# The token parts of a decoder's last gated projection: 384 and 160 columns instead of 256 and 288

## The chip, the cores and the metric

The kernel runs on one core of one Trainium2 chip. The time is device microseconds of that core, for one launch that does one inference step. The kernel before takes 2436.96 us (median of three runs, 2435.14 to 2437.22).

## What is computed

Two layers of a decoder trunk over 544 tokens (512 of a prompt, 8 x 4 of running samples), width 1024. A layer is a half-step SwiGLU, a mixer of three branches, a second half-step SwiGLU and a gated embedding. Only the last of these matters here, in the second layer, with the final norm behind it:

```python
h = rmsnorm(x, w['g_ple'])
x = x + jax.nn.sigmoid(h @ w['w_ple_gate']) * (p @ w['w_ple_proj'])
...
y_prompt = rmsnorm(yp, g_final)
y_sample = rmsnorm(ys, g_final)
```

`w_ple_gate` is 1024 x 1024, `w_ple_proj` is 256 x 1024, and `rmsnorm` divides each token by the root of its mean square over the 1024 channels.

## The kernel before

Activations lie transposed: channels on the 128 partitions, 544 tokens along the columns, in eight tiles `x[0]` to `x[7]`. Weights are blocks of 128 x 128 and are the stationary operand; the tokens stream. To keep f32 accuracy, every operand is split in a high and a low half (f32r), and a product is three matmuls that add up in PSUM: low weights with high tokens, high with high, high with low (`mm` in line 1066). Each of these matmuls is issued with a weight load of its own, also where two in a row use the same weights.

In most of the kernel a product streams the 544 tokens as two halves of 272 columns (lines 302 and 325). The last function, `ple_last` (from line 1053), instead takes the tokens in two parts, so that the final norm and the output of the first part can be done while the second part is computed. `parts` is in blocks of 128 tokens: (0, 2) is columns 0 to 255, (2, 5) is columns 256 to 543. It has these steps, each for a part `h` and a block of 128 output channels `m`:

- `gate(h, m)`: 8 blocks x 3 = 24 matmuls (line 1069), then VectorE multiplies by the norm (L1087) and ScalarE takes the sigmoid (L1088).
- `proj(h, m)`: 2 x 3 = 6 matmuls (L1069); VectorE multiplies with the gate (L1095) and adds to `x` (L1096); ScalarE squares the result (L1098, L1100); VectorE adds the squares up in `acc` (L1101).
- `norm_sum(h)`: for each block of 128 tokens a one-column matmul (L516, plain f32, two passes) sums `acc` over the partitions; a few tiny VectorE operations and a square root on ScalarE (L502, with a table load) make the inverse root; VectorE scales one identity block for each block of tokens (L523).
- `norm_bc(h)`: for each block a matmul with 128 columns (32 for the last) spreads the result over the partitions (L530, two passes); ScalarE copies it to `rstd` (L532, and L534 for the last 32 columns).
- `out(h, m)`: VectorE scales `x` (L1114) and a DMA on SP's or ScalarE's queue (L1116) writes the part's columns.

The order is written out by hand. Part 0: four gates interleaved, with the norm of the incoming `x` among them, then `proj(0, m)` and `gate(0, m + 4)` in turn, and the last four `proj`. Weights are split once, in part 0, and stay in SBUF for part 1. Part 1: `gate(1, 0)`, `gate(1, 1)`, `proj(1, 0)`, `gate(1, 2)`, `norm_sum(0)`, `proj(1, 1)`, `gate(1, 3)`, `norm_bc(0)`, `proj(1, 2)`, then the rest, two `out(0, ...)` behind each of four `proj`. At the end `norm_sum(1)`, `norm_bc(1)` and eight `out(1, m)`. PSUM is four tiles of two banks that are taken in turn (`bank`), so a group of matmuls must wait until the group four before it has been read.

Of the kernel before, what the change touches and what calls it, by code (L numbers as in the profile page):

```python
# [102 lines left out]
class Kern:  # L103
# [950 lines left out]
    def ple_last(self, l, inp):  # L1054
        nc = self.nc
        xg = inp.tiles
        pp, _ = self.pp_in
        self.extra = EXTRA[6]
        self.keep = True
        wg, wp, ts = {}, {}, {}  # L1060
        parts = ((0, 2), (2, 5))
        rms = {}

        def span(h):
            return slice(parts[h][0] * P, min(parts[h][1] * P, T))

        def mm(ps, w, xs, c, first, last):
            for i, (a, b) in enumerate(((w[1], xs[0]), (w[0], xs[0]), (w[0], xs[1]))):
                nc.tensor.matmul(ps, a, b[:, c], start=first and i == 0, stop=last and i == 2)  # L1069

        def acc_mm(h, store, name, m, xs):
            pst, = self.bank(1)
            c = span(h)
            ps = pst[:, 0, :c.stop - c.start]
            for k in range(len(xs)):
                if h == 0:
                    store[k, m] = self.take(name, l, k, m)
                mm(ps, store[k, m], xs[k], c, k == 0, k == len(xs) - 1)
            return ps

        def gate(h, m, ps=None):
            c = span(h)
            if ps is None:
                ps = acc_mm(h, wg, "w_ple_gate", m, xg)
            t_ = ts[h, m] = self.slot()
            t = t_[0][:, c]
            nc.vector.tensor_mul(t, ps, self.rstd[:, c])  # L1087
            nc.scalar.activation(t, t, AF.Sigmoid)  # L1088

        def proj(h, m):  # L1090
            c = span(h)
            ps = acc_mm(h, wp, "w_ple_proj", m, pp)
            t_ = ts.pop((h, m))
            t, x = t_[0][:, c], self.x[m][:, c]
            nc.vector.tensor_mul(t, ps, t)  # L1095
            nc.vector.tensor_add(x, x, t)  # L1096
            if m == 0:
                nc.scalar.activation(self.acc[:, c], x, AF.Square)  # L1098
            else:
                nc.scalar.activation(t, x, AF.Square)  # L1100
                nc.vector.tensor_add(self.acc[:, c], self.acc[:, c], t)  # L1101
            self.drop(t_)

        def norm_sum(h):
            rms[h], = self.bank(1)
            self.rms_sum(rms[h][:, 0, :], *parts[h])

        def norm_bc(h):
            self.rms_bc(rms[h], *parts[h])

        def out(h, m):
            c = span(h)
            t = self.slot()
            nc.vector.scalar_tensor_tensor(t[0][:, c], self.x[m][:, c], self.par[:, PB_GF + m:PB_GF + m + 1],  # L1114
                                           self.rstd[:, c], op0=ALU.mult, op1=ALU.mult)
            (nc.scalar if m % 2 else nc.sync).dma_start(out=self.outs["yT"][m][:, c], in_=t[0][:, c])  # L1116
            self.drop(t)

        c = span(0)
        pst = self.bank(2)  # L1120
        ps4 = [pst[i // 2][:, i % 2, :c.stop - c.start] for i in range(4)]
        hooks = dict(zip(LAST_AT, (f for _, f in self.rms_hooks())))
        for n in range(4 * KD):
            k, i = divmod(n, 4)
            wg[k, i] = self.take("w_ple_gate", l, k, i)
            mm(ps4[i], wg[k, i], xg[k], c, k == 0, k == KD - 1)
            if n in hooks:
                hooks[n]()
        self.flush()
        for m in range(4):  # L1130
            gate(0, m, ps4[m])
        for m in range(KD):
            proj(0, m)
            if m + 4 < KD:
                gate(0, m + 4)
        gate(1, 0)
        for m in range(KD):
            if m + 1 < KD:
                gate(1, m + 1)
            if m == 1:  # L1140
                norm_sum(0)
            if m == 2:
                norm_bc(0)
            proj(1, m)
            if 2 <= m < 6:
                out(0, 2 * m - 4)
                out(0, 2 * m - 3)
        norm_sum(1)
        norm_bc(1)
        for m in range(KD):  # L1150
            out(1, m)
# [120 lines left out]
```

## Time and profile before

| | |
|---|---|
| median of three runs | 2436.96 us |
| span of the profiled execution | 2435.3 us |
| TensorE matmuls busy | 2414.3 us |
| VectorE busy | 1903.0 us |
| ScalarE busy | 1087.3 us |
| weight loads and matmuls | 19016 each |
| of these, in `ple_last` (L1069) | 480: 240 of 256 columns, 240 of 288 |

The profile gives one time for the profiled execution, its span from the first to the last instruction; it lies 1.7 us below the median of the runs and 0.2 us above the shortest. Of the 2435.3 us, `ple_last` fills the last 80.5, from 2354.8 on. Busy times of TensorE are those of pipelined instructions with modelled ends: one matmul is shown with some 290 ns though the next one starts 125 ns later.

### The profile page before, as it was taken

The page shows a single profiled execution, that of the slowest core. Times are in us where ns is not written, and L with a number is a line of the kernel's source. Part 1 is how long each engine was busy: PE and PEld are TensorE (multiplying, and loading weights), DVE is VectorE, ACT ScalarE, POOL GpSimd, SP SyncE. Part 2 cuts the span into 40 slices and gives each one's busy share as a digit, 9 for nine tenths or more (in the row PEclk, how much of TensorE's full clock was granted, in tenths as well). Part 3 has the DMA queues.
Part 4 walks back from the last instruction along what each step waited for, and adds up shares of the span by engine and source line. Part 5 has one row for each costly group of instructions (what it writes and reads, how often), then busy time and mean ns, then how long its engine had stood idle before and what let it go on. Part 6 is the DMA issues. An engine that isn't in the chain of part 4 may idle for free.

```text
span 2435.3 us, 48371 instructions
## 1 busy us (share of the span) xinstructions
PE 2414.3 (99%) x19016; PEld 2401.5 (99%) x19016; DVE 1903.0 (78%) x3583; ACT 1087.3 (45%) x2021; POOL 202.0 (8%) x248
## 2 busy tenths in 40 slices
PE   8999999999999999999999999999999999999997
PEld 8999999999999999999999999999999999999997
DVE  7887776778788887878788777866788779877775
ACT  6443444444446444435554444434354454434352
POOL 1111000010110100100010110000011011101000
PEclk9999999999999999999999999999999999999998
DMA  6665551354554555555255565523455536656521
GB/s 199 143 148 140 148 163 58 88 143 118 145 158 114 141 144 145 148 139 157 63 139 142 135 157 137 161 70 82 128 133 146 165 91 145 157 131 154 145 80 38
DMA packets 173988, 318.79 MB, mean 131 GB/s; under 512 B 19584, under 2 KB 21888, under 8 KB 173760
## 3 DMA queue, kind: packets, MB, share of 16 engines
q1 hardware_dynamic: 139248, 252.24, 34.2%
q0 software_dynamic: 32640, 61.16, 15.0%
q8 instruction: 149, 2.44, 0.4%
q10 hardware_dynamic: 1872, 2.29, 0.3%
q14 instruction: 79, 0.65, 0.1%
HBM read 312.63 MB, written 2.99 MB: 130 GB/s over the span
## 4 chain that ended last, share of the span: by engine, by line
PE 99%; DVE 0%; ACT 0%; DMA 0%; issue 0%; DVEq 0%; ACTq 0%
PE ps L325 47%; PE ps L302 46%; PE ps L807 2%; PE ps L1069 2%; PE ps L530 0%; PE ps L516 0%; PE ps L972 0%; DMA par<-in_par 0%; DVE s L1114 0%; PE ps L974 0%; DVE x L1096 0%; ACT s L1100 0%; ACT L502 0%; ACT L244 0%; DVE s L1095 0%
## 5 line engine op out<-in xcount | busy, mean ns | idle before, releaser
L325 PE MATMUL ps<-s,s 128*128 128x272 f32 x9156 | 1162.0, 288 | 0.0
L325 PEld LDWEIGHTS ps<-s,s 128*128 128x128 f32 x9156 | 1153.5, 188 | 0.4 <-DVE s L938 0.2
L302 PE MATMUL ps<-s,s 128*128 128x272 f32 x8880 | 1132.6, 288 | 7.3 <-ACT s L443 7.3
L302 PEld LDWEIGHTS ps<-s,s 128*128 128x128 f32 x8880 | 1121.7, 189 | 7.6 <-ACT s L443 7.2
L244 ACT ACTIVATE s<-s 128x512 fp32r<-128x512 f32 x1169 | 663.1, 621 | 506.0 <-DVE s L237 461.6
L249 DVE TENSOR_TENSOR s<-s,s 128x512 fp32r<-128x512 f32 x1169 | 768.3, 685 | 8.6 <-ACT s L244 8.6
L231 POOL DMA_DIRECT2D s<-in_wts x218 | 186.0, 854 | 1738.2 <-DMA s<-in_wts 448.5
L660 DVE SCALAR_TENSOR_TENSOR x<-ps,x 128x544 f32<-128x544 f32 x128 | 92.4, 722 | 137.2 <-PE ps L302 137.0
L579 ACT ACTIVATE s<-ps 128x272 f32<-128x272 f32 x109 | 43.2, 396 | 251.3 <-PE ps L325 251.1
L237 DVE TENSOR_TENSOR s<-s,s 128x512 f32<-128x512 f32 x218 | 149.3, 685 | 0.0
L581 DVE TENSOR_TENSOR s<-ps,s 128x272 f32<-128x272 f32 x109 | 48.0, 441 | 69.5 <-PE ps L325 43.3
L587 DVE TENSOR_TENSOR s<-ps,s 128x272 f32<-128x272 f32 x109 | 48.1, 441 | 63.8 <-PE ps L325 62.7
L607 ACT ACTIVATE s<-s 128x544 f32<-128x544 f32 x88 | 57.9, 658 | 89.4 <-DVE s L620 89.0
L613 ACT ACTIVATE s<-s 128x544 fp32r<-128x544 f32 x88 | 57.6, 654 | 59.8 <-DVE s L610 44.1
L864 DVE TENSOR_TENSOR s<-ps,s 128x544 f32<-128x544 f32 x48 | 34.8, 725 | 50.7 <-PE ps L302 46.2
L616 DVE TENSOR_TENSOR s<-s,s 128x544 fp32r<-128x544 f32 x88 | 63.2, 718 | 5.9 <-ACT s L613 5.8
L1069 PE MATMUL ps<-s,s 128*128 128x256 f32 (+1 forms) x480 | 61.6, 289 | 1.8 <-ACT rstd L532 1.8
L623 DVE TENSOR_TENSOR s<-s,rstd 128x544 f32<-128x544 f32 x88 | 63.2, 718 | 0.1
L1069 PEld LDWEIGHTS ps<-s,s 128*128 128x128 f32 x480 | 60.5, 188 | 2.0 <-ACT rstd L532 2.0
L610 DVE TENSOR_TENSOR s<-s,s 128x544 f32<-128x544 f32 x82 | 58.9, 718 | 0.4
L858 ACT ACTIVATE s<-s 128x544 f32<-128x544 f32 x48 | 29.0, 652 | 67.6 <-DVE s L593 67.6
L620 DVE TENSOR_TENSOR s<-s,rstd 128x544 f32<-128x544 f32 x82 | 59.0, 719 | 0.0
(133 smaller groups left out, 1176.4 us busy)
## 6 DMA issues: line engine op xcount, KB each, us to landing
s<-in_wts SPq DMA_DIRECT2D x951, 256.0 KB, 3.4
s<-in_wts POOLq DMA_DIRECT2D x218, 256.0 KB, 4.6
x<-in_xT ACTq DMA_DIRECT2D x4, 272.0 KB, 5.2
x<-in_xT SPq DMA_DIRECT2D x4, 272.0 KB, 4.8
s<-in_pT POOLq DMA_DIRECT2D x4, 272.0 KB, 3.2
out_yT<-s SPq DMA_DIRECT2D x4, 144.0 KB, 1.8
out_yT<-s ACTq DMA_DIRECT2D x4, 144.0 KB, 1.8
s<-in_st_in POOLq DMA_DIRECT2D x2, 272.0 KB, 3.1
```

The lines of the kernel that those rows point to most:

```text
L231: self.nc.gpsimd.dma_start(out=t, in_=src(1 if w == "R1" else 2, 4), accum_op=ALU.add)
L237: self.nc.vector.tensor_add(self.new_raw(w, u0, 2 if w == "R3" else 1), self.read_raw(a, u0), self.read_raw(b, u0))
L244: self.nc.scalar.activation(a[0][:, :UC], self.read_raw(w, u0), AF.Copy)
L249: self.nc.vector.tensor_sub(lo, self.read_raw(w, u0), hi.bitcast(F32))
L302: self.nc.tensor.matmul(ps[:, h, :HT], a, bh, start=first and i == 0, stop=last and i == 2)
L325: self.nc.tensor.matmul(ps, a, b, start=first and i == 0, stop=last and i == 2)
L610: nc.vector.tensor_mul(o[:, :], o[:, :], t[:, :])
L616: nc.vector.tensor_sub(lo, o[:, :], hi.bitcast(F32))
L620: nc.vector.tensor_mul(t[:, :], t[:, :], self.rstd[:, :])
L623: nc.vector.tensor_mul(o[:, :], o[:, :], self.rstd[:, :])
L660: nc.vector.scalar_tensor_tensor(xm, self.pv(pst[i]), 0.5, xm, op0=ALU.mult, op1=ALU.add)
L1069: nc.tensor.matmul(ps, a, b[:, c], start=first and i == 0, stop=last and i == 2)
```

## The change

One table of two pairs: the border between the token parts moves by one block of 128 tokens. Part 0 is now columns 0 to 383, part 1 columns 384 to 543.

```diff
         wg, wp, ts = {}, {}, {}
-        parts = ((0, 2), (2, 5))
+        parts = ((0, 3), (3, 5))
         rms = {}
```

The number of matmuls and weight loads and their order stay. What changes are the widths of all operations in `ple_last` and the number of blocks in the two norms. Two places on TensorE show it. The first is `norm_sum(0)`, between `gate(1, 2)` (ahead) and `proj(1, 1)` (behind), before:

```order
-L1069 MATMUL ps_71<-s_4614_29706,s_4583_29519 128x288
-L1069 MATMUL ps_71<-s_4615_29707,s_4583_29519 128x288
-L516 MATMUL ps_72<-ones,acc 128x1 x2
-L1069 MATMUL ps_73<-s_4548_29348,s_4592_29560 128x288
-L1069 MATMUL ps_73<-s_4548_29348,s_4591_29559 128x288
```

At the same place with the change (`s_...` are SBUF slots, `ps_71` to `ps_74` the four PSUM tiles):

```order
+L1069 MATMUL ps_71<-s_4614_29706,s_4583_29519 128x160
+L1069 MATMUL ps_71<-s_4615_29707,s_4583_29519 128x160
+L516 MATMUL ps_72<-ones,acc 128x1 x3
+L1069 MATMUL ps_73<-s_4548_29348,s_4592_29560 128x160
+L1069 MATMUL ps_73<-s_4548_29348,s_4591_29559 128x160
```

The first norm sums three blocks instead of two, at the same place between the same neighbours, whose slots and PSUM tiles are the same. The second place is the end of TensorE's work, the last projection and the second norm, before:

```order
-L1069 MATMUL ps_72<-s_4551_29354,s_4622_29737 128x288
-L1069 MATMUL ps_72<-s_4552_29355,s_4622_29737 128x288
-L516 MATMUL ps_73<-ones,acc 128x1 x3
-L530 MATMUL ps_73<-s_4650_30393,ones 128x128 x2
-L530 MATMUL ps_73<-s_4650_30393,ones 128x32
```

And with the change:

```order
+L1069 MATMUL ps_72<-s_4551_29354,s_4622_29737 128x160
+L1069 MATMUL ps_72<-s_4552_29355,s_4622_29737 128x160
+L516 MATMUL ps_73<-ones,acc 128x1 x2
+L530 MATMUL ps_73<-s_4650_30395,ones 128x128
+L530 MATMUL ps_73<-s_4650_30395,ones 128x32
```

The last norm has two blocks instead of three. Each of these rows of L516 and L530 is two weight loads and two matmuls on the chip.

## Rows read from the trace of the kernel before

**Rows 1.** The page: span; TensorE's share; granted clock in 40 slices

```profile
span 2435.3 us, 48371 instructions
...
PE 2414.3 (99%) x19016; PEld 2401.5 (99%) x19016; DVE 1903.0 (78%) x3583; ACT 1087.3 (45%) x2021; POOL 202.0 (8%) x248
...
PEclk9999999999999999999999999999999999999998
```

**Rows 2.** Stages of `ple_last`: length, busy (count) by engine, granted clock, DMA

```profile
2354.80:2385.40 30.60, 30.60 (x262) 30.60 (x261) 17.08 (x43) 12.10 (x25) 0.00 (x0) 1.00 0.01 2
2385.40:2395.60 10.20, 10.20 (x79) 10.20 (x79) 5.21 (x13) 2.59 (x6) 0.00 (x0) 1.00 0.00 0
2395.60:2403.30 7.70, 5.97 (x47) 5.73 (x45) 4.30 (x15) 4.40 (x8) 0.00 (x0) 1.00 0.01 2
2403.30:2420.40 17.10, 17.03 (x126) 16.80 (x126) 10.35 (x24) 3.43 (x8) 0.00 (x0) 1.00 0.18 62
2420.40:2435.30 14.90, 2.93 (x12) 2.71 (x12) 7.06 (x22) 2.85 (x6) 0.00 (x0) 0.57 0.23 79
```

**Rows 3.** Timeline, matmuls of four widths: start, us, engine, line, operands, count

```profile
2354.84 4.76 PE L1069 MATMUL ps<-s,s 128*128 128x256 f32 x39
...
2339.80 10.44 PE L302 MATMUL ps<-s,s 128*128 128x272 f32 x82
...
433.65 27.22 PE L807 MATMUL ps<-s,s 128*128 128x512 f32 x117
...
2403.33 17.03 PE L1069 MATMUL ps<-s,s 128*128 128x288 f32 x126 [1.76 <-ACT rstd L532]
```

**Rows 4.** Timeline, narrow matmuls and their weight loads; last, the load after the hole

```profile
2359.33 1.20 PEld L516 LDWEIGHTS ps<-ones,acc 128*128 128x128 f32 x10
...
665.43 1.05 PE L972 MATMUL ps<-wst,s 128*128 128x128 f32 x8
...
2403.33 0.30 PEld L1069 LDWEIGHTS ps<-s,s 128*128 128x128 f32 x2 [2.00 <-ACT rstd L532]
```

**Rows 5.** Window of the spatial matmuls (128 and 32 columns), as rows 2

```profile
665.30:671.00 5.70, 5.70 (x43) 5.06 (x41) 5.06 (x12) 2.52 (x4) 0.00 (x0) 1.00 0.07 12
```

**Rows 6.** Timeline, ScalarE around the first part's norm

```profile
2396.91 1.28 ACT L502 ACT_TABLE_LOAD   x1
...
2401.27 1.28 ACT L1088 ACT_TABLE_LOAD   x1
...
2402.91 0.37 ACT L532 ACTIVATE rstd<-ps 128x256 f32<-128x256 f32 x1
```

**Rows 7.** Timeline of the tail

```profile
2418.81 0.46 DVE L1087 TENSOR_TENSOR s<-ps,rstd 128x288 f32<-128x288 f32 x1 [0.45 <-PE ps L1069]
...
2423.41 1.44 PE L516 MATMUL ps<-ones,acc 128*128 128x1 f32 x6 [3.05 <-DVE acc L1101]
...
2426.67 1.49 PE L530 MATMUL ps<-s,ones 128*128 128x128 f32 x6 [1.82 <-DVE s L523]
...
2428.70 3.52 DVE L1114 SCALAR_TENSOR_TENSOR s<-x,par,rstd 128x288 f32<-128x288 f32 x8 [1.74 <-ACT rstd L534]
2429.68 2.91 ACTq L1116 DMA_DIRECT2D out_yT<-s  x4
```

**Rows 8.** Groups from 2300 on, by shape: count, busy us, mean ns, idle before

```profile
L1096 DVE TENSOR_TENSOR x<-x,s 128x288 f32<-128x288 f32 x8 | 3.7, 459 | 0.3
...
L1114 DVE SCALAR_TENSOR_TENSOR s<-x,par,rstd 128x288 f32<-128x288 f32 x8 | 3.5, 511 | 1.7 <-ACT rstd L534 1.7
L1114 DVE SCALAR_TENSOR_TENSOR s<-x,par,rstd 128x256 f32<-128x256 f32 x8 | 3.5, 480 | 0.0
L1096 DVE TENSOR_TENSOR x<-x,s 128x256 f32<-128x256 f32 x8 | 3.4, 425 | 0.3
...
L1100 ACT ACTIVATE s<-x 128x288 f32<-128x288 f32 x7 | 3.1, 443 | 7.2 <-DVE x L1096 7.2
...
L1100 ACT ACTIVATE s<-x 128x256 f32<-128x256 f32 x7 | 2.9, 419 | 7.2 <-DVE x L1096 7.2
```

## The prediction, made before the change was run

> **What bounds the kernel now.** Read the page first: TensorE is busy for 99% of the span, and the granted clock stands at full speed in all slices but the last [rows 1]. So the time is the number of matmuls times the pace of one, plus the few stretches in which TensorE waits. The second view is the table by stage of the last function [rows 2]: part 0 (256 columns) fills 30.6 us without a gap, part 1 (288 columns) follows from 2385.4, there is one hole of 1.7 us (7.70 us with 5.97 busy, where the first part's norm is made), and from 2420.4 on a tail of 14.9 us in which TensorE does 2.93 us of work. The third view is the timeline of TensorE alone, for the pace of a matmul by its width [rows 3]. A matmul's own duration (280 to 300 ns) is latency; the pace is (busy time less one duration) divided by (count less one). For 256 columns (4.76 - 0.28)/38 = 118 ns; for 272, (10.44 - 0.29)/81 = 125 ns; for 288, (17.03 - 0.30)/125 = 134 ns; for 512, (27.22 - 0.39)/116 = 231 ns. From 256 to 512 this is close to a straight line, 0.44 ns a column. If it were straight for all widths, 384 + 160 columns would cost what 256 + 288 cost.
>
> The question is whether it stays straight below 256, and the fourth view answers that: what narrow matmuls cost when each brings its own weights [rows 4]. The loads for ten one-column matmuls take (1.20 - 0.19)/9 = 112 ns each; eight matmuls of 128 columns run at (1.05 - 0.27)/7 = 111 ns. One column and 128 columns cost the same: the 128x128 weight load sets the pace, not the columns. Those are plain f32 operands. For the operands of this projection there is one look: after the hole the first weight load has nothing before it, and two loads together take 0.30 us, the second itself 0.19, so the second began 0.11 us behind the first (last row of rows 4), at a time when no earlier matmul could hold it up. So a load takes some 110 ns here too; at 256 columns (118 ns) it is only just hidden, at 160 columns it is not.
>
> **The change, part by part.** The same 480 matmuls and weight loads run in the same order; the order of the instructions shows only other widths, and that the first norm takes three blocks of 128 tokens instead of two and the last one two instead of three.
>
> *Part 0, 240 matmuls from 256 to 384 columns.* No row has 384. Per column the 256 row gives 0.462 ns and the 512 row 0.452, so it lies between 173.5 and 177.3 ns; I take the straight line between both, 175. The stage also holds the 20 matmuls of the incoming norm at 112 ns, 2.2 us, which stay. Before: 30.6 us. After: 240 x 0.175 + 2.2 = 44.2. **+13.6 us** (13.2 to 14.2). Nothing hides it: TensorE has no gap in this stage. VectorE (17.1 us busy of 30.6) and ScalarE (12.1) grow with the columns by less than half and stay under 44.
>
> *Part 1 up to the norm, 78 matmuls from 288 to 160 columns* (two gates of 24, the first projection of 6, the third gate of 24). Streaming 160 columns would, on the line, take 118 - 96 x 0.44 = 76 ns; the load takes 112. The larger counts. I take 112 (108 to 115, the 0.11 us of the first load and a little for the hand-over). 10.2 us become 78 x 0.112 = 8.7, **-1.5**. VectorE enters this stage late, since each of the last four projections of part 0 leaves it and ScalarE a chain of some 2.2 us at 384 columns (three operations of 0.56 and a square of 0.53, on the line of the widths in [rows 8]) while TensorE needs only 4.2 us for all four; but it reads their PSUM tiles some 8.4 us after the last gate of part 0, and TensorE wants the last of them back only after 10.2 us (4.2 + 48 x 0.112 + 6 x 0.112). That cover is 1.8 us.
>
> *The hole.* It is set by ScalarE, not by matmuls: the table load for the square root, the root, the small VectorE chain, the scaled identity blocks, one projection step, the second table load, the sigmoid and the copy of the norm out of PSUM, which TensorE waits for [rows 6]. The two table loads of 1.28 us stay. One more block for the norm adds 0.22 us to its sums and 0.24 to the blocks; the copy grows from 256 to 384 columns, about 0.1; five steps of VectorE and ScalarE shrink from 288 to 160 columns. From [rows 8] such a step goes from 0.46 to 0.32 us on VectorE (459 at 288, 425 at 256: 1.06 ns a column) and from 0.44 to 0.34 on ScalarE (443 and 419). 7.7 us become about 7.2, **-0.5**; TensorE still waits some 1.7 us of it.
>
> *Part 1 after the norm to the last gate, 114 matmuls.* They take 15.5 us now, from 2403.33 to the VectorE step that reads the last gate at 2418.81 [rows 7], at 134 ns each and with the first load and the last latency around them. Each becomes 112: 114 x 0.022 = **-2.5**. VectorE must keep up: a step of 30 matmuls will take 3.35 us. Its work in it is four operations with the wait for the square, 0.35 + 0.35 + 0.36 + 0.35 with their issue, from 0.67 us behind the gate on, and in three of them two output scalings of 384 columns (480 at 256, 511 at 288: about 0.60 at 384, overlapped to 0.52 [rows 8]): some 3.1 us. Just covered; if not, at most 3 x 0.3 = 0.9 us come on top.
>
> *The tail*, from that VectorE step at 2418.81 to the end of the span, 16.5 us. The gate's product and two projection steps run in a row on VectorE and ScalarE: 4.6 us to the first norm matmul at 2423.41; with 160 columns 0.67 for the six matmuls of the first projection and eight operations of 0.32 to 0.35, 3.4 in all: -1.2. The sums: 4 matmuls instead of 6; they run at 0.21 us, since the mean granted clock of the stage is 0.57, so most of it at the lower level, 1.2 GHz, after TensorE stood idle: -0.4. The broadcast: 4 instead of 6, likewise -0.4. The copy to SBUF: -0.1. The eight last scalings: 3.52 us at 288, spaced 0.43; at 256 spaced 0.40, so at 160 about 0.30 with 0.39 for the last: 2.5, -1.0. The last transfer's landing: 80 KB instead of 144, at most -0.1. With the hand-overs between them **-3.3** (2.8 if the landing and the copy give nothing and the steps shrink less; 3.8 if the clock stays up because TensorE idles for a shorter time before the sums).
>
> Sum: 13.6 - 1.5 - 0.5 - 2.5 - 3.3 = **+5.8 us**. The profiled execution has a span of 2435.3 us, 1.7 below the median of the runs, 2436.96; I take the 1.7 as common to both kernels and put the sum on the median: **2442.8 us**, 0.24% more.
>
> A rule that speaks against this sum: the Trainium skill, page "TensorE: Matmul & The Clock Gate", section "Back-to-back issue gap", gives 81 ns at 128 columns and 131 ns at 512 for a stream of weight load and matmul pairs; an estimate from these two puts 160 columns at 85 ns, and the kernel near the next rival's time. The trace of this case does not agree: it has 231 ns at 512 and 111 at 128 [rows 3, 4].
>
> **The rivals.**
> (a) *The weight load is hidden at 160 columns after all*, because loads of this operand type run ahead in a steady stream and the 0.11 us after the hole was the latency of a first load. Then the pace is 76 ns. Up to the norm 78 x 0.076 = 5.9, -4.3; the hole stays with ScalarE, -0.5; after the norm TensorE would need 2.3 us a step and VectorE's 2.8 to 3.1 would bind: three steps of 2.8 and one of 2.3 give 10.7 instead of 15.1, -4.4; tail -3.3. Sum 13.6 - 12.5 = +1.1: 2438.1 us, no change. This is the case in which it is not slower; it decides from a load time under about 80 ns. For it: the plain f32 rows are another operand type. Against it: 0.11 us for the one load of this type that stands alone.
> (b) *The granted clock falls to 1.2 GHz in part 1*, at the hole or before it. At that level a pair takes 0.21 us (six take 1.44 us in [rows 7]); 228 matmuls would cost 22 us more, 2465 us. Against it: eight-packs of 128 columns with small gaps ran for 5.7 us at a granted clock of 1.00 [rows 5], and so did the hole of 1.7 us.
> (c) *VectorE becomes the bound* after the norm, by its two wide scalings a step, or the PSUM tiles come back late at the border of the parts (cover 1.8 us): up to 0.9 + 1 us more, 2444.7 us. For it: the margin of 0.2 us a step. Against it: PSUM has four tiles in turn, so a late step is made good by the three without scalings.
>
> **How the numbers follow.** Forecast 0.80, (a) 0.13, (b) 0.04, (c) 0.03. About 0.2% (4.9 us) is what a measurement of this kernel can tell from no change, and the forecast's own range, 2441.0 to 2444.6 (384 columns at 173.5 or 177.3 ns, loads at 108 or 115, tail 2.8 or 3.8, not all at one end together), crosses it: of its 0.80 I put 0.60 above and 0.20 within. With (b) and (c) slower, (a) mostly within: slower 0.67, same 0.31, faster 0.02. The range for 8 in 10 takes in (a) and (c) but not (b): 2437.6 to 2445.0 us.
>
> **What would show it.** In the profile after: the 384-column stretch at 175 ns a matmul and 44 us long; the 160-column stretch at 110 to 114 ns with weight loads back to back, whatever the columns; the hole still there and still ended by the copy of the norm; a tail of 13.2 us from the last gate's product. Wrong would be: a pace under 90 ns at 160 columns (rival a), a granted clock under 1.00 before the last matmul (b), TensorE waiting for VectorE's reads of PSUM in part 1 (c), or 384 columns off the line.

## The result, and the profile after

| | before | the change |
|---|---|---|
| median of five runs | 2436.96 us | 2454.64 us |
| lowest and highest | 2435.14, 2437.22 | 2441.82, 2454.79 |
| ratio, 95% interval | | 1.0063 [1.0045, 1.0082] |

The change is slower, outside the predicted range, and its runs do not scatter about a middle: one took 2441.82 us, four took 2454.50 to 2454.79. The profiled execution is the one of 2441.82 us, with a span of 2440.1. It is the one that shows what the columns do; what the other four did is not in it. The page of this profile, against [rows 1]:

```profile
span 2440.1 us, 48371 instructions
...
PE 2421.6 (99%) x19016; PEld 2409.0 (99%) x19016; DVE 1903.3 (78%) x3583; ACT 1086.6 (45%) x2021; POOL 201.4 (8%) x248
...
PEclk9999999999999999999999999999999999999999
```

TensorE has 7.3 us more busy time, VectorE and ScalarE the same; the clock row has no 8 left in the last slice. The stages of the last function in the same execution, against [rows 2] (length, busy time and count by engine, granted clock, DMA):

```profile
2354.00:2398.20 44.20, 44.20 (x261) 44.20 (x261) 20.61 (x44) 13.60 (x25) 0.00 (x0) 1.00 0.00 1
2398.30:2406.80 8.50, 8.50 (x78) 8.50 (x78) 5.25 (x12) 2.48 (x6) 0.00 (x0) 1.00 0.00 0
2406.80:2414.20 7.40, 5.68 (x51) 5.53 (x50) 3.67 (x16) 4.15 (x8) 0.00 (x0) 1.00 0.01 2
2414.30:2428.30 14.00, 14.00 (x126) 14.00 (x126) 9.12 (x24) 2.49 (x8) 0.00 (x0) 1.00 0.30 108
2428.30:2440.10 11.80, 2.06 (x11) 1.69 (x9) 5.41 (x21) 2.53 (x6) 0.00 (x0) 0.62 0.20 62
```

Part 0 takes 44.2 us instead of 30.6, part 1 and the tail are shorter, the hole (7.4 us with 5.68 busy) is still there, and the clock is at 1.00 until the tail. The timeline of this execution gives the paces and the steps of the tail, against [rows 3, 7] (start, us, engine, line, operands, count):

```profile
2353.95 7.01 PE L1069 MATMUL ps<-s,s 128*128 128x384 f32 x39
...
2406.96 0.76 PE L516 MATMUL ps<-ones,acc 128*128 128x1 f32 x6
...
2414.26 14.30 PE L1069 MATMUL ps<-s,s 128*128 128x160 f32 x126 [1.78 <-ACT rstd L532]
...
2427.26 0.32 DVE L1087 TENSOR_TENSOR s<-ps,rstd 128x160 f32<-128x160 f32 x1 [0.20 <-PE ps L1069]
...
2430.72 0.74 PE L516 MATMUL ps<-ones,acc 128*128 128x1 f32 x4 [2.16 <-DVE acc L1101]
...
2434.77 2.46 DVE L1114 SCALAR_TENSOR_TENSOR s<-x,par,rstd 128x160 f32<-128x160 f32 x8 [1.40 <-ACT rstd L534]
```

384 columns run at (7.01 - 0.34)/38 = 176 ns, 160 columns at (14.30 - 0.27)/125 = 112 ns.

### The profile page after: what moved, and what is told of

It reads as the page before. It is cut to its first block, busy times and chain, and to the rows that moved or that the text cites. A ratio compares the mean times of both kernels' runs of the same rounds, so it can differ in the third digit from the quotient of the medians.

```text
span 2440.1 us, 48371 instructions
## 1 busy us (share of the span) xinstructions
PE 2421.6 (99%) x19016; PEld 2409.0 (99%) x19016; DVE 1903.3 (78%) x3583; ACT 1086.6 (45%) x2021; POOL 201.4 (8%) x248
## 4 chain that ended last, share of the span: by engine, by line
PE 99%; DVE 0%; ACT 0%; DMA 0%; issue 0%; ACTq 0%; DVEq 0%
PE ps L325 47%; PE ps L302 46%; PE ps L1069 3%; PE ps L807 2%; PE ps L516 0%; PE ps L530 0%; PE ps L972 0%; DMA par<-in_par 0%; PE ps L974 0%; DVE s L1114 0%; ACT L502 0%; ACT L244 0%; ACT s L1100 0%; DVE x L1096 0%; DVE s L523 0%
## 5 line engine op out<-in xcount | busy, mean ns | idle before, releaser
L302 PE MATMUL ps<-s,s 128*128 128x272 f32 x8880 | 1132.0, 288 | 7.0 <-ACT s L443 7.0
L302 PEld LDWEIGHTS ps<-s,s 128*128 128x128 f32 x8880 | 1121.1, 189 | 7.3 <-ACT s L443 7.0
L613 ACT ACTIVATE s<-s 128x544 fp32r<-128x544 f32 x88 | 57.5, 654 | 59.7 <-DVE s L610 44.2
L1069 PE MATMUL ps<-s,s 128*128 128x384 f32 (+1 forms) x480 | 70.2, 307 | 1.8 <-ACT rstd L532 1.8
```

Of the source, the lines that this page charges most:

```text
L302: self.nc.tensor.matmul(ps[:, h, :HT], a, bh, start=first and i == 0, stop=last and i == 2)
```

## The experiments

All ran with the kernel before beside them, on one chip per group of runs; its runs there lie between 2435.7 and 2437.9 us. Each run is one execution.

| label | edit | runs | times, us | ratio to the kernel before, 95% interval |
|---|---|---|---|---|
| e1, with the first five | the change as it is | 12 | 4 at 2441.8 to 2442.1; 8 at 2452.7 to 2454.9 | e1: 1.0049 [1.0032, 1.0067] |
| e2 | no hole | 11 | 2440.6 to 2442.4 | 1.0020 [1.0011, 1.0029] |
| e3 | part 1 streams 256 columns | 7 | 6 at 2443.1 to 2443.4; 2444.5 | 1.0027 [1.0017, 1.0037] |
| e4 | part 1 streams 224 columns | 8 | 6 at 2442.0 to 2442.4; 2 at 2444.0 | 1.0024 [1.0014, 1.0033] |
| e5, e10 | one gate behind the hole streams 256 | 15 | 5 at 2441.9 to 2442.4; 10 at 2443.7 to 2444.9 | 1.0025 [1.0016, 1.0035], 1.0029 [1.0018, 1.0041] |
| e6 | all gates and projections but one ahead of the hole stream 256 | 6 | 3 at 2443.0 to 2443.3; 3 at 2452.6 to 2455.5 | 1.0047 [1.0030, 1.0063] |
| e7 | the kernel before | 10 | 2436.7 to 2438.0 | 1.0001 [0.9991, 1.0010] |
| e8 | the kernel before without the hole | 11 | 2434.5 to 2435.6 | 0.9991 [0.9983, 1.0000] |
| e9 | as e8, one DMA on another queue | 11 | 2434.1 to 2435.0 | 0.9991 [0.9982, 1.0000] |

### The change once more (e1)

No edit.

> The change once more, without an edit, to see how its executions spread. Theory A (the granted clock falls to 1.2 GHz at the hole in part 1, where TensorE waits for the copy of the first norm, and stays there for the matmuls of 160 columns behind it): the executions fall in two groups, one near 2441.8 us and one about 126 x (0.213 - 0.112) = 12.8 us above it, near 2454.6, and a trace of the second group shows 112 ns a pair up to the hole and 213 ns from it to the end. Theory B (the narrow stretch itself makes the clock fall, at a place of its own, with no need of the hole): the times lie spread between 2441 and 2465 us, and a trace shows the pace change to 213 ns away from the hole.

Seven runs: 2441.99, 2442.00, 2442.10 and 2452.67, 2454.73, 2454.73, 2454.85 us. This time the profiled execution is one of the upper group, span 2453.0. Its stages (the third is the hole, the fourth the 126 matmuls behind it):

```profile
2398.70:2407.30 8.60, 8.60 (x79) 8.60 (x79) 5.26 (x12) 2.48 (x6) 0.00 (x0) 1.00 0.00 0
2407.30:2414.60 7.30, 5.60 (x51) 5.44 (x49) 3.67 (x16) 4.15 (x8) 0.00 (x0) 1.00 0.01 2
2414.80:2441.60 26.80, 26.80 (x126) 26.78 (x126) 9.44 (x24) 2.73 (x9) 0.00 (x0) 0.50 0.16 59
2441.60:2453.00 11.40, 2.27 (x9) 1.85 (x8) 5.09 (x20) 2.20 (x6) 0.00 (x0) 0.50 0.19 58
```

And its TensorE timeline around the hole:

```profile
2408.00 3.56 PE L1069 MATMUL ps<-s,s 128*128 128x160 f32 x30
...
2412.02 0.88 PE L1069 MATMUL ps<-s,s 128*128 128x160 f32 x6
2414.66 27.13 PE L1069 MATMUL ps<-s,s 128*128 128x160 f32 x126 [1.76 <-ACT rstd L532]
```

Its last function begins 0.4 us later; from there to the end of the hole it takes what the other execution took, to a few hundredths: 30 matmuls in 3.56 us, a wait of 1.76 us for the copy of the norm. Behind the hole the granted clock is 0.50, that is 1.2 GHz, and it stays there until the end, though TensorE has no further gap in those 26.8 us. The pairs take (27.13 - 0.42)/125 = 214 ns instead of 112: 126 x 0.102 = 12.8 us, and the two spans differ by 12.9. So this execution of the upper group is one of the lower group with the clock lost behind the hole. Theory A's numbers hold; whether the hole or the narrow matmuls do it is for the next runs.

### The change without the hole (e2)

```diff
         def norm_bc(h):
+            if h == 0:
+                rms[h], = self.bank(1)
             self.rms_bc(rms[h], *parts[h])
...
-            if m == 2:
+            if m == 3:
                 norm_bc(0)
             proj(1, m)
-            if 2 <= m < 6:
-                out(0, 2 * m - 4)
-                out(0, 2 * m - 3)
+            if 3 <= m < 7:
+                out(0, 2 * m - 6)
+                out(0, 2 * m - 5)
```

> The change with the hole taken away: the broadcast of the first norm takes a PSUM tile of its own and comes one projection later, so that no group of matmuls waits for the copy; the outputs of part 0 follow one step later. Theory A: TensorE runs through part 1 without a gap, the clock stays at 1.00 up to the last projection, all executions are near 2441.8 - 1.8 = 2440 us. Theory B: the hole's 1.8 us are saved, but executions above 2450 us remain, most of them as with the change, and their mean granted clock is below 0.995.

Eleven runs, none above 2442.4 us. The stage table of its part 1 and two rows of its timeline:

```profile
2399.00:2427.00 28.00, 28.00 (x253) 28.00 (x252) 16.99 (x50) 9.35 (x21) 0.00 (x0) 1.00 0.12 41
2427.00:2440.20 13.20, 2.34 (x11) 1.96 (x9) 6.47 (x23) 2.53 (x6) 0.00 (x0) 0.62 0.26 85
```

```profile
2427.96 1.14 DVE L1116 SCALAR_TENSOR_TENSOR s<-x,par,rstd 128x384 f32<-128x384 f32 x2
...
2430.48 1.02 PE L516 MATMUL ps<-ones,acc 128*128 128x1 f32 x4 [3.22 <-DVE acc L1101]
```

28.0 us with 253 matmuls (the 240 of 160 columns, the twelve of the norm and the last of part 0) without a gap and at a clock of 1.00. So the narrow matmuls do not make the clock fall by themselves, in any of eleven runs; theory B is out. The 2 us expected did not show in the time, though. The outputs moved one step later, two scalings of 384 columns (1.14 us) now stand between VectorE's last two projections, and TensorE waits 3.22 us for the last sums where it waited 2.16. The sums take 1.02 us instead of 0.74, all of them at a granted clock of 0.50, which costs another 0.3. And the last function begins 0.7 us later in this execution than in the profiled one of the change (2354.66 against 2353.95), which has nothing to do with the edit (see e7).

### More columns in all of part 1 (e3, e4)

The parts stay; the matmuls of part 1 stream the last 256 (224) of the 544 columns, and the product that is read is the last 160 of these. The first 96 (64) are computed a second time and dropped.

```diff
             c = span(h)
+            if h == 1:
+                c = slice(T - 256, T)
             ps = pst[:, 0, :c.stop - c.start]
...
-            return ps
+            return pst[:, 0, 96:256] if h == 1 else ps
```

> The change with its parts kept, but every matmul of part 1 streams 256 columns, 288 to 543, of which the first 96 are computed a second time and not read. The hole stays. A pair then takes 118 ns as in the rows of the kernel before, not 112, so 240 x 0.006 = 1.5 us more than the good executions of the change: 2443.3 us. Theory A, with the hole alone as the cause: executions in two groups as with the change, the upper one near 2443.3 + 126 x (0.213 - 0.118) = 2455 us. Theory A with the narrow stream as the second condition, or theory B: all executions near 2443.3 us, clock 0.998.

> As the run with 256 streamed columns, but 224 (columns 320 to 543, the first 64 computed a second time and not read). On the line of the wider rows 224 columns stream in 104 ns, under the 112 ns of the weight load, so the pairs should still take 112 ns and the good executions 2441.8 us. If the number of streamed columns has no part in the fall of the clock (theory A, hole alone): two groups, 2441.8 and 2454.6 us. If the narrow stream has a part in it: most or all executions in the lower group.

With 256 columns six of seven runs are at 2443.1 to 2443.4 us, one at 2444.5; with 224, six of eight at 2442.0 to 2442.4 and two at 2444.0. No run of either is near 2454. The profile with 256 shows no fall ahead of the tail. The one with 224 caught one of the two upper runs:

```profile
2408.20 3.59 PE L1069 MATMUL ps<-s,s 128*128 128x224 f32 x30
...
2414.87 15.96 PE L1069 MATMUL ps<-s,s 128*128 128x224 f32 x126 [1.74 <-ACT rstd L532]
```

```profile
2407.50:2414.80 7.30, 5.62 (x51) 5.44 (x49) 3.67 (x16) 4.14 (x8) 0.00 (x0) 1.00 0.01 2
2415.10:2418.40 3.30, 3.30 (x17) 3.30 (x17) 1.36 (x3) 0.00 (x0) 0.00 (x0) 0.50 0.32 119
2418.60:2430.60 12.00, 12.00 (x110) 12.00 (x108) 7.78 (x21) 2.36 (x7) 0.00 (x0) 1.00 0.26 94
```

First, 30 matmuls of 224 columns took 3.59 us, as 30 of 160 took 3.56: the 64 columns more are free, since the weight load sets the pace. Second, the clock fell at the hole here too (0.50 from 2415.1 on), but it was back at 1.00 within 3.5 us. That costs 17 pairs at the lower clock, 1.7 us, and not 126. So the fall behind the hole does not need 160 columns; what the width changes is whether the clock comes back. How often the clock falls may depend on the width too: runs with a time of the upper kind are two of eight with 224 columns and one of seven with 256, and 18 of 27 where 160 columns run ahead of the hole (e1 with the first five, e5, e10).

### The kernel before, again (e7)

No edit. Theory A2, which the next texts name, is the reading reached so far: the hole lets the clock fall in some executions, and the matmuls behind it settle whether it comes back.

> The kernel before, without an edit, for another trace. Its runs lie between 2435.7 and 2437.7 us. Theory A2: the upper ones have a fall of the clock at the same hole, from which 288-column matmuls bring it back after a few us, at a cost of about 1.7 us; a trace near 2437.4 us shows a stretch of granted clock below 1.00 behind the hole, a trace near 2435.8 shows none before the tail. Rival: both kinds of run have a clock of 1.00 up to the tail, and the spread is elsewhere.

The profiled execution took 2437.59 us. From the hole on:

```profile
2395.20:2402.80 7.60, 5.85 (x46) 5.62 (x44) 4.30 (x15) 4.41 (x8) 0.00 (x0) 1.00 0.01 2
2402.80:2404.30 1.50, 1.49 (x11) 1.49 (x12) 1.18 (x3) 0.29 (x1) 0.00 (x0) 1.00 0.00 0
2404.40:2407.70 3.30, 3.30 (x16) 3.30 (x15) 0.00 (x0) 0.00 (x0) 0.00 (x0) 0.50 0.23 79
2407.80:2421.10 13.30, 13.30 (x102) 13.30 (x101) 8.78 (x21) 3.11 (x7) 0.00 (x0) 1.00 0.18 60
```

The kernel before loses the clock behind the same hole, 1.6 us after its end, and it is back 3.4 us later, under 288-column matmuls. Its 126 matmuls behind the hole take 18.52 us instead of 17.03 [rows 3]: 1.5 us.

That is a part of the 2 us by which its own runs differ, but not all of it. Another part is set at the very start: in the twelve traces of this document the same run of 192 matmuls (L302) begins between 34.80 us (e6) and 35.94 us (the kernel before), and the last function begins 2318.8 to 2318.9 us behind them in every one. So an execution is up to 1.2 us longer or shorter by its first 36 us. In every run listed with its span, the time is 1.6 to 1.8 us above the span. The first profiled execution of the kernel before (span 2435.3) therefore took about 2437.0 us, as long as the upper ones of its runs and not as short as the shortest, and yet it has no fall behind the hole. That the runs below 2436.2 us have no fall was expected, but none of them was profiled; it is not shown.

### Only ahead of the hole, only behind it (e6, e5, e10)

```diff
             c = span(h)
-            ps = pst[:, 0, :c.stop - c.start]
+            w = 256 if h == 1 and name == "w_ple_gate" and m == 4 else c.stop - c.start
+            c = slice(c.stop - w, c.stop)
+            ps = pst[:, 0, :w]
...
-            return ps
+            return pst[:, 0, 96:256] if w == 256 and h == 1 else ps
```

This is e5, and e10 again for another trace. In e6 the condition is `(m < 4 if name == "w_ple_gate" else m < 2)`: the four gates and two projections ahead of the hole.

> The change, but the one gate directly behind the hole (24 matmuls) streams 256 columns, 96 of them computed a second time and not read; all other matmuls of part 1 keep 160. Theory A2 (the hole lets the clock fall in some executions, and 160-column pairs, which hold the clock when it is up, do not bring it back when it is down): the wider gate brings it back, the rest holds it; all executions lie between 2442.0 us (no fall; 24 x 0.006 = 0.1 us more) and about 2445 us (24 pairs at 0.23 instead of 0.12), none near 2454. Rival (the clock stays down after a fall for a reason other than the width of what follows): executions near 2454.6 remain in most runs.

> The counterpart: the four gates and two projections of part 1 ahead of the hole stream 256 columns, all behind it keep 160. Theory A2: it is what follows the hole that counts, so two groups remain, near 2442.5 us (108 x 0.006 = 0.6 more than the change's lower group, partly inside the hole) and 12.8 us above. Rival (it is the narrow stretch ahead of the hole that makes the clock fall there): all executions in the lower group.

> The change with the one gate behind the hole widened to 256 columns, without another edit, for a trace of an execution in which the clock fell. Theory A2: all executions between 2441.9 and 2445 us; a trace near 2444.6 shows a granted clock of 0.50 behind the hole that is back at 1.00 before or soon after the wide gate ends, and 112 ns a pair from there. Rival: an execution near 2454.

256 columns ahead of the hole do not help: three of six runs are at 2452.6 to 2455.5. In its trace the clock is up for 2 us behind the hole, falls then, and stays down:

```profile
2414.40:2416.50 2.10, 2.06 (x18) 2.06 (x19) 1.38 (x3) 0.22 (x1) 0.00 (x0) 1.00 0.04 16
2416.60:2439.30 22.70, 22.70 (x109) 22.70 (x108) 8.04 (x21) 2.50 (x8) 0.00 (x0) 0.50 0.18 67
```

One gate of 256 columns behind the hole is enough: none of 15 runs is above 2444.9 us, where the change as it is has eight of twelve above 2452. The trace of e5 (2442.29 us) has no fall ahead of the tail. The trace of e10 (2444.0 us) shows how the gate works (the gate runs from 2414.81, for 4.0 us):

```profile
2414.80:2416.30 1.50, 1.49 (x12) 1.49 (x13) 1.28 (x3) 0.18 (x1) 0.00 (x0) 1.00 0.00 0
2416.40:2419.70 3.30, 3.30 (x18) 3.30 (x16) 0.33 (x2) 0.25 (x1) 0.00 (x0) 0.50 0.32 119
2419.80:2430.60 10.80, 10.80 (x99) 10.80 (x98) 7.46 (x20) 2.02 (x6) 0.00 (x0) 1.00 0.29 106
```

The clock fell in the middle of the gate, was at 0.50 from 2416.4 to 2419.7, and back at 1.00 at 2419.8; the 160-column pairs that follow hold it for the remaining 10.8 us. Theory A2 is what these runs show: within some 2 us behind the hole the clock may fall; what is issued there settles whether that costs 2 us or 13. In all three traces of a fall in which 224 to 288 columns followed, the clock came back within 3.5 us; in both traces in which 160 columns followed, it did not in 23 and 27 us.

### The kernel before without its hole (e8, e9)

The edit is that of e2, on parts (0, 2) and (2, 5), with the last pair of outputs behind the last projection (`if 3 <= m < 6`, then `out(0, 6)` and `out(0, 7)` ahead of `norm_sum(1)`). In e9 the DMA of that last output goes to SP's queue:

```diff
-            (nc.scalar if m % 2 else nc.sync).dma_start(out=self.outs["yT"][m][:, c], in_=t[0][:, c])
+            (nc.scalar if m % 2 and (h, m) != (0, 7) else nc.sync).dma_start(out=self.outs["yT"][m][:, c], in_=t[0][:, c])
```

> The kernel before, with its parts of 256 and 288 columns, and the hole taken away: the broadcast of the first norm on a PSUM tile of its own and one projection later, its outputs one step later, and the last pair of them in the idle time of VectorE behind the last projection. Expected: TensorE without a gap up to the last projection, 1.8 to 2 us less, and no fall of the clock before the tail: 2433.8 to 2434.5 us in all runs, some 2.5 us under the median of the kernel before. If the last pair of outputs does not fit in the idle time, up to 0.9 us of that is lost.

> The kernel before without the hole, as in the run before, but the transfer of the last output tile of part 0 goes out on SP's queue instead of ScalarE's. In the run before that DMA stood ahead of the last square root's table load on ScalarE and made it wait for VectorE: the load began 1.65 us after the last square (2421.61 against 2419.48 + 0.44) where it otherwise follows at once, and the last broadcast came 0.76 us later behind the sums than in the kernel before (4.02 against 3.26). Expected: 0.7 us less than 2434.85, that is 2434.1 us, in one group. If VectorE's two scalings themselves are what delays the sums, nothing changes.

e8: median 2434.85 us, 2.2 under the kernel before beside it (2437.07), and above the 2433.8 to 2434.5 expected; part 1 up to the last projection is one stretch at full clock:

```profile
2394.70:2417.20 22.50, 22.50 (x173) 22.49 (x171) 13.58 (x37) 7.93 (x15) 0.00 (x0) 1.00 0.11 36
```

The tail lost 0.8 us of the gain, because ScalarE could not start the table load of the root until VectorE had made the output that a DMA ahead of it in its queue waits for. The two rows are e8's square and its table load, and below them e9's, where the load follows the square at once:

```profile
2419.48 0.44 ACT L1100 ACTIVATE s<-x 128x288 f32<-128x288 f32 x1 [1.39 <-DVE x L1096]
...
2421.61 1.28 ACT L502 ACT_TABLE_LOAD   x1 [1.68 <-DVE s L1116]
```

```profile
2420.31 0.44 ACT L1100 ACTIVATE s<-x 128x288 f32<-128x288 f32 x1 [1.39 <-DVE x L1096]
2420.77 1.28 ACT L502 ACT_TABLE_LOAD   x1
```

e9's median is 2434.64, only 0.2 lower, with overlapping runs (2434.12 to 2435.00 against 2434.54 to 2435.55): the wait is gone from the trace, but the 0.7 us expected are not shown by the times. Its highest of eleven runs, 2435.00, lies under the lowest of the 17 runs of the kernel before beside it, 2435.87, so it is faster than that kernel, if only by 0.1%.

## Why the prediction was wrong, step by step

**Part 0**: +13.6 forecast; from 2353.95 to 2398.3 it is 44.3 us against 30.6, +13.7. 384 columns at 176 ns, 175 forecast.

**Part 1 up to the norm**: 8.7 us forecast, 8.66 measured (2398.3 to 2406.96), -1.5. The weight load sets the pace at 112 ns, as forecast from one exposed load and two rows of plain f32 operands. Rival (a), that it is hidden, would have been 76 ns; e4 excludes it from the other side, since a pace set by the columns would have grown from 160 to 224 columns. The Trainium skill's page "TensorE: Matmul & The Clock Gate", section "LDWEIGHTS (loading the stationary operand)", gives for the time of a load in ns the number of the weights' columns divided by 1.2; for 128 columns an estimate from that is 107 ns. The trace comes near it, with 112 a pair. The 81 ns a pair at 128 columns that the Trainium skill gives on the same page, section "Back-to-back issue gap", and that the prediction weighed, is not borne out here: 111 ns at 128 columns [rows 4].

**The hole**: 7.2 us forecast, 7.3 measured (2406.96 to 2414.26). **Behind it**: -2.5 forecast, 13.0 instead of 15.5 us. **The tail**: -3.3 forecast, 12.8 instead of 16.5 us, -3.6; the sums started with the clock still up (four in 0.74 us), the case that the prediction had at its end of 3.8. The sum of the measured terms is +5.7; the span of this execution is 4.8 longer, since the last function began 0.9 us earlier in it, by the first 36 us of the program (see e7). Its time of 2441.82, and the lower group as a whole (2441.8 to 2442.1), lie 1 us under the forecast of 2442.8.

**Where it failed** is the clock behind the hole: the term of -2.5 us for part 1 after the norm took the granted clock to stay at 1.00, and the fall of the clock, rival (b), was given a chance of 0.04 and a wrong price. In the upper group the clock is at 0.50 there, and the 114 matmuls of that term take 0.102 us each more, so that it comes to about +9.1. The prediction said that against a fall stood the hole itself, which had run at a granted clock of 1.00, and the packs of 128-column matmuls. That was one execution. In e7 the same kernel loses the clock behind the same hole, so one trace could not bear that weight. (Its three times, 2435.14 beside 2436.96 and 2437.22, were no clear sign of it: the profiled execution, without a fall, took about 2437.0.) The packs of 128 columns had no hole of 1.8 us ahead of them, so they say that narrow matmuls hold a clock that is up, which e2 confirms over 28 us; they say nothing on whether such matmuls bring it back. The price was 22 us, for all 228 matmuls. The clock falls behind the hole, so at most 126 pairs pay 0.102 us each, 12.8. With that price and the eight of twelve runs in which it happened, the median is the upper group's, 2454.6, outside the range that left this rival out.

Rival (c) did not occur: TensorE's only wait in part 1 is the one for the copy of the norm, as before. The direction, slower, was right.

What stays open: why the clock falls behind this hole in some executions and not in others of the same kernel, what it is in the wider matmuls that brings it back, and whether 160-column pairs would have brought it back in a longer stretch than the 27 us that were seen. One hint on the first, and no more: the four runs of the change in the lower group lie within 0.3 us, though the first 36 us alone can shift a run by 1.2, so whether the clock falls may hang on when the hole comes.

## What to carry to other kernels

Splitting work along the streamed columns keeps its total only as long as each part streams longer than its weights load; here 160 and 224 columns cost the same 112 ns, and 256 cost 118. Where TensorE waits between two stretches, look at what follows the wait, not only at the wait: a fall of the clock behind the same hole cost 2 us where matmuls of 224 to 288 columns came next and 13 us where 160 columns did, and the cure was to remove the wait or to put one wide group behind it. One trace in which the clock stays up does not show that it always does: when the runs of a kernel form two groups, take a trace of each before weighing the risk.

## What was not expected of the hardware

A wait of TensorE of 1.5 to 1.8 us was followed, 0.1 to 2.1 us behind its end, by a granted clock of 1.2 GHz in five of the nine traces that have such a hole (e1, e4, e6, e7, e10), of both kernels; the other four are those of before, of the change, of e3 and of e5. Behind it TensorE can be busy without a gap for 27 us, with a weight load under way all the time, and the clock stays at 0.50 (e1), while the same matmuls keep a clock of 1.00 for 28 us if there was no hole (e2). The weight load slows with the clock: the pair that takes 112 ns at 1.00 takes 214 ns at 0.50, and 160 columns alone, at twice the 76 ns of the prediction's line, would by that estimate take only 152.
